# Other SBUF phases for the matmul operands of a feed-forward: slots, weight sums and gated tiles moved by unused columns

## The chip, the cores and the metric

The kernel runs on one core of a Trainium2 chip. The metric is the device time of one execution in microseconds (us). Three runs of the kernel before took 2018.37, 2019.25 and 2019.88 us, so the median is 2019.25 us.

## The reference, cut to what matters

Two layers over 512 tokens of width 1024, in f32. Each layer has a feed-forward, a mixer (a convolution module in layer 0, sparse attention in layer 1), a second feed-forward and a gated embedding; a last norm follows.

```python
def swiglu(x, wg, wu, wd):
    return (jax.nn.silu(x @ wg) * (x @ wu)) @ wd

for i in range(DEPTH):                                   # DEPTH = 2
    x = x + 0.5 * swiglu(rms_norm(x, ffn1_norm[i]), ffn1_w_gate[i], ffn1_w_up[i], ffn1_w_down[i])
    h = rms_norm(x, mix_norm[i])
    x = x + (conformer_conv(h, ...) if i % 2 == 0 else nsa_mixer(h, ...))
    x = x + 0.5 * swiglu(rms_norm(x, ffn2_norm[i]), ffn2_w_gate[i], ffn2_w_up[i], ffn2_w_down[i])
    gate = jax.nn.sigmoid(rms_norm(x, ple_norm[i]) @ ple_w_gate[i])
    x = x + gate * (p[i] @ ple_w_in[i])
return rms_norm(x, final_norm)
```

The gate and up matrices are 1024 x 2816, the down matrix 2816 x 1024; there are four feed-forwards in all.

## The kernel before, in words

**Numbers.** Activations lie transposed: 128 features on the partitions, 512 tokens along the row. An f32 product is made of three matmuls in fp32r: every operand is split into a high part h and a low part l, and `mm3` adds h·h (line L356), h·l (L357) and l·h (L358) in PSUM. In a name like `b<-s,wh` of the profile, `b` is the PSUM bank, the first name after the arrow is the moving operand (the activations, streamed through the array) and the second the stationary one (128x128 weights, loaded into the array ahead of the stream). Weight halves are `wh` and `wl`. A load of weights and a stream of another matmul run at the same time.

**The tiles.**
- `s`: 24 slots of 512 f32 (2048 bytes) in the pool `slots`. They hold the residual stream, and the h and l halves of the normed input of most matrices (`X`).
- `px`: tiles of 1024 f32 in the pool `phase`: in a feed-forward the sums of input quarters (`right_sums`), h in the first half and l in the second; in the gated embedding its normed input.
- `raw`, `rawx`: weights as loaded. `wh`, `wl`: their halves, five buffers of 4096 bytes each, eight 128x128 blocks to a buffer. `s1hl`: h and l of a sum of weights, in one tile. `sq`: other sums of weights.
- `G`: products of gate and up before and after the gate. `hid`: h and l of the gated hidden tiles, the moving operand of the down matrix.

**The feed-forward.** `ffn` works in three parts of 8, 8 and 6 hidden tiles (`PARTS`). The first two hidden tiles of the first part are plain products with 512-wide matmuls (moving `s`). The others go two by two through `pairs`, a Strassen-Winograd scheme with seven products of half size for each of gate and up, all 256 tokens wide. A product is four blocks deep, so 4 x 3 = 12 matmuls; a pair of hidden tiles takes 14 products or 168 matmuls: six products with moving `s` (72 matmuls; products "s" and the first of "d"), six with moving `px` and stationary `wh`/`wl` (72; products "c" and the second of "d"), two with moving `px` and stationary `s1hl` (24; product "e"). The order within a pair is: s, s (both halves), c with T2, e with T1, c with T3, d with B22 (moving `s`), d with T4. There are 3 + 4 + 3 pairs in a feed-forward, 40 in the kernel. After each part the down matrix follows, 512 wide, moving `hid`: 22 x 8 x 3 x 4 = 2112 matmuls.

**Elsewhere** `s` is the moving operand of 512-wide matmuls in the plain products, the convolution's first matrix and the attention's projections, `px` in the gated embedding.

**Order.** A scheduler sets the order of instructions on each engine while the program is built; weights run ahead of the matmuls by five buffers (`HLB`). SBUF addresses come from the pools: each pool lies behind the one opened before it, and within a pool each tag behind the tag first asked for before it. A pool's tile with a new tag therefore moves everything behind it.

Of the kernel before, what the change touches and what calls it, by code (L numbers as in the profile page):

```python
# [11 lines left out]
F32 = mybir.dt.float32  # L12
# [9 lines left out]
TAPS = 31  # L22
X_W1, WARM = 4, 18
OUTS = 2
CONV_FIN = 0
PE_LATE = (3, 4, 5)
FIN_PRI = 100
# [24 lines left out]
G, HPG, HD, KV, QD = 4, 4, 64, 256, 1024  # L52
# [143 lines left out]
class Kern:  # L196
    def __init__(self, ctx, tc, aps):
        self.ctx, self.tc, self.nc = ctx, tc, tc.nc
        self.a = aps
        pool = lambda name, **kw: ctx.enter_context(tc.tile_pool(name=name, **kw))  # L200
        self.cpool = pool("consts", bufs=1)
        self.wpool = pool("weights", bufs=1)
        self.spool = pool("slots", bufs=1)
        self.tiny = pool("tiny", bufs=2)
        self.ppool = pool("ps", bufs=1, space=PSUM)
        self.dpool = pool("dram", bufs=1, space=DRAM)
        self.uid = 0
        self.raw, self.hl, self.sums = {}, {}, {}
        self.unskewed = []
        self.HLB, self.held, self.now = 5, set(), None  # L210
        self.next_raw = self.next_split = 0
# [8 lines left out]
        return self.ptile("t", self.tb, dt=dt)  # L220

    def ptile(self, tag, n, w=512, dt=F32):
        self.uid += 1
        return self.phase.tile([128, w], dt, name=f"{tag}{self.uid}", tag=tag, bufs=n)

# [605 lines left out]
    def conv(self, nxt):  # L831
# [24 lines left out]
        for c in range(KD):  # L856
# [13 lines left out]
            for p, o in ((pa, c), (pg, c + KD)):  # L870
                for k in range(KD):
                    self.mm3(p, self.block(("conv_w_pw1", 0, k, o)), X[k], k == 0, k == KD - 1)
                if c == 1 and p is (pa, pg)[CONV_FIN]:
                    next(fin)
# [501 lines left out]
    def final(self, X, R, Z):  # L1376
# [6 lines left out]
        def norm(hs, squares):  # L1383
# [15 lines left out]
            for m in range(KD):  # L1399
                if m % OUTS == 0:  # L1400
                    pair = self.ptile("hid", HIDS).rearrange("p (m n) -> p m n", n=256)
                x, o = self.xs[m][:, hs], pair[:, m % OUTS]
                if m == OUT_AFTER:
# [3 lines left out]
                with self.tc.issue_after((self.root if m in OUT_POOL else self.vins) if m >= OUT_AFTER else done):  # L1407
                    if m in OUT_POOL:
                        nc.gpsimd.tensor_tensor(o, x, Rf, op=OP.mult)
                    else:  # L1410
                        nc.vector.scalar_tensor_tensor(o, x, self.col("final_norm", m), p, op0=OP.mult, op1=OP.mult)
                if m % OUTS == OUTS - 1:
                    nc.sync.dma_start(out[:, m + 1 - OUTS:m + 1, hs], pair[:, :OUTS])
            yield
# [24 lines left out]

    def run(self):  # L1440
        def phase():
            return self.tc.tile_pool(name="phase", bufs=1, reuse_waits="tile")

        self.zd = [self.dpool.tile([D, S], F32, name=f"z{i}") for i in range(L)]
        self.load_consts()
        for i in range(L):
            self.tb = 4
            with phase() as self.phase:
                if i == 0:
                    self.prep_start("ffn1_norm", 0)  # L1450
                    for k in range(KD):
                        self.parts(k)
                    with self.tc.issue_after(self.parted[0]), self.tc.issue_after(self.parted[1]):
                        for k in range(KD):
                            self.square_sum(k)
                self.ffn(1, i, ("mix_norm", i))
            self.tb = 7 if i == 0 else NTB
            with phase() as self.phase:
                if i == 0:
                    self.conv(("ffn2_norm", i))  # L1460
                    self.bias_tables()
                else:
                    self.nsa(("ffn2_norm", i))
            self.tb = 4
            with phase() as self.phase:
                self.ffn(2, i, ("ple_norm", i))
                self.ple(i, ("ffn1_norm", 1) if i == 0 else ("final_norm", 0))
# [64 lines left out]
```

## Time and profile before

| | |
|---|---|
| time of three runs | 2018.37, 2019.25, 2019.88 us |
| the profiled execution: device time / span | 2018.77 us / 2016.7 us |
| granted TensorE clock, mean | 0.996 |
| TensorE matmul (PE) busy | 1992.7 us, 99% |
| weight load (PEld) busy | 1789.7 us, 89% |
| VectorE (DVE) busy | 1546.0 us, 77% |
| ScalarE (ACT) busy | 1100.5 us, 55% |
| GpSimd (POOL) busy | 330.7 us, 16% |
| DMA | 117 GB/s |

The span is the time from the first to the last instruction of the program; the device time has 2.1 us around it. A matmul's duration in the profile is its modelled way through the array, so that it is longer than its share of the time: successive matmuls overlap. What a matmul costs in a stream is the distance from its start to the next one's start.

### The profile page before, as it was taken

How to read it: one execution, taken by the hardware profiler on the slowest of the kernel's cores; microseconds unless marked ns; L12 is line 12 of the kernel's file. 1: busy time of each engine (PE TensorE's matmuls, PEld its weight loads, DVE VectorE, ACT ScalarE, POOL GpSimd, SP SyncE). 2: the span in 40 equal slices, each digit the busy share in tenths (PEclk: the TensorE clock that was granted, in tenths of full speed). 3: DMA queues.
4: the chain of work that ended last, by engine and by line, in shares of the span. 5: the costliest groups of instructions: out<-in, count | busy, mean ns of one | idle time of the engine just before them, and what ended most of it. 6: DMA issues, size and time to landing. Idle time of an engine off the chain costs nothing.

```text
span 2016.7 us, 32709 instructions
## 1 busy us (share of the span) xinstructions
PE 1992.7 (99%) x12534; PEld 1789.7 (89%) x12534; DVE 1546.0 (77%) x2703; ACT 1100.5 (55%) x1972; POOL 330.7 (16%) x365
## 2 busy tenths in 40 slices
PE   8999999999999999999999999999999999999998
PEld 7989999888789898988999989888888789998987
DVE  8869777795687796777968868646889797786875
ACT  7535445662665363555644535437888665363543
POOL 0000000352300000012000000557666200000022
PEclk9999999999999999999999999999999999999999
DMA  4323323466425244243232322463333023232241
GB/s 170 105 96 104 126 74 105 180 206 202 141 97 166 86 144 136 97 133 118 84 115 95 115 87 90 162 182 116 95 90 104 25 99 120 95 116 94 94 141 59
DMA packets 79483, 235.16 MB, mean 117 GB/s; under 512 B 8848, under 2 KB 16160, under 8 KB 79328
## 3 DMA queue, kind: packets, MB, share of 16 engines
q1 hardware_dynamic: 78368, 230.69, 34.6%
q8 instruction: 98, 1.61, 0.3%
q0 software_dynamic: 816, 2.33, 0.3%
q14 instruction: 57, 0.47, 0.1%
q10 hardware_dynamic: 144, 0.07, 0.0%
HBM read 214.66 MB, written 16.29 MB: 115 GB/s over the span
## 4 chain that ended last, share of the span: by engine, by line
PE 91%; DVE 6%; ACT 2%; issue 1%; DMA 0%; SPq 0%; POOL 0%; DVEq 0%; POOLq 0%; ACTq 0%
PE b L356 28%; PE b L357 27%; PE b L358 27%; PE b L821 2%; PE b L1180 1%; PE b L1244 1%; PE b L1263 1%; PE b L1119 1%; PE b L1264 1%; DVE s L415 1%; DVE t L482 1%; DVE wl L294 1%; DVE px L491 0%; DVE acc L432 0%; DMA raw<-in_w 0%
## 5 line engine op out<-in xcount | busy, mean ns | idle before, releaser
L356 PE MATMUL b<-s,wh 128*128 128x256 f32 (+1 forms) x1408 | 448.8, 320 | 0.6 <-ACT wh L292 0.5
L357 PE MATMUL b<-s,wh 128*128 128x256 f32 (+1 forms) x1408 | 447.5, 318 | 0.9 <-DVE s L415 0.6
L358 PE MATMUL b<-s,wl 128*128 128x256 f32 (+1 forms) x1408 | 446.3, 319 | 0.2 <-DVE wl L294 0.2
L292 ACT ACTIVATE wh<-raw 128x1024 fp32r<-128x1024 f32 (+1 forms) x251 | 263.7, 1054 | 256.5 <-PE b L357 174.1
L357 PE MATMUL b<-px,wh 128*128 128x256 f32 (+1 forms) x1112 | 321.5, 289 | 1.7 <-DVE px L491 1.7
L356 PE MATMUL b<-px,wh 128*128 128x256 f32 (+1 forms) x1112 | 321.4, 290 | 0.7 <-ACT G L503 0.7
L358 PE MATMUL b<-px,wl 128*128 128x256 f32 (+1 forms) x1112 | 321.5, 289 | 0.0
L294 DVE TENSOR_TENSOR wl<-raw,wh 128x1024 fp32r<-128x1024 f32 (+1 forms) x205 | 251.0, 1226 | 68.9 <-ACT wh L292 68.4
L356 PEld LDWEIGHTS b<-s,wh 128*128 128x128 f32 x1408 | 268.3, 191 | 19.2 <-ACT wh L292 1.1
L357 PEld LDWEIGHTS b<-s,wh 128*128 128x128 f32 x1408 | 268.0, 190 | 19.5 <-DVE s L415 1.9
L358 PEld LDWEIGHTS b<-s,wl 128*128 128x128 f32 x1408 | 267.5, 191 | 17.7 <-DVE wl L294 0.5
L358 PE MATMUL b<-hid,wl 128*128 128x512 f32 x704 | 275.3, 393 | 0.0
L357 PE MATMUL b<-hid,wh 128*128 128x512 f32 x704 | 274.5, 391 | 0.0
L356 PE MATMUL b<-hid,wh 128*128 128x512 f32 x704 | 269.7, 390 | 0.0
L294 POOL TENSOR_TENSOR wl<-raw,wh 128x1024 fp32r<-128x1024 f32 (+1 forms) x53 | 128.5, 2431 | 709.8 <-ACT wh L292 709.6
L503 ACT ACTIVATE G<-b 128x256 f32<-128x256 f32 x400 | 145.1, 377 | 141.7 <-PE b L358 122.6
L357 PEld LDWEIGHTS b<-px,wh 128*128 128x128 f32 x1112 | 209.5, 188 | 7.0 <-DVE px L491 2.1
L356 PEld LDWEIGHTS b<-px,wh 128*128 128x128 f32 x1112 | 209.5, 189 | 6.0 <-ACT G L503 1.3
L358 PEld LDWEIGHTS b<-px,wl 128*128 128x128 f32 x1112 | 209.4, 188 | 3.8
L357 PEld LDWEIGHTS b<-hid,wh 128*128 128x128 f32 x704 | 132.2, 188 | 29.4
L356 PEld LDWEIGHTS b<-hid,wh 128*128 128x128 f32 x704 | 132.2, 188 | 28.1
L358 PEld LDWEIGHTS b<-hid,wl 128*128 128x128 f32 x704 | 132.1, 188 | 27.5
(246 smaller groups left out, 3624.4 us busy)
## 6 DMA issues: line engine op xcount, KB each, us to landing
raw<-in_w SPq DMA_DIRECT2D x255, 512.0 KB, 3.3
rawx<-in_w SPq DMA_DIRECT2D x80, 512.0 KB, 3.3
tw<-in_tw SPq DMA_DIRECT2D x20, 576.0 KB, 6.8
skew<-table SPq DMA_DIRECT2D x16, 320.0 KB, 5.8
z<-t SPq DMA_DIRECT2D x16, 256.0 KB, 2.2
hid<-z SPq DMA_DIRECT2D x16, 256.0 KB, 4.1
tt<-skew SPq DMA_DIRECT2D x16, 256.0 KB, 3.0
wr<-in_w SPq DMA_DIRECT2D x8, 512.0 KB, 4.1
```

The lines of the kernel that those rows point to most:

```text
L292: nc.scalar.activation(h[:, c], t[:, c], AF.Copy)
L294: eng.tensor_tensor(l[:, c], t[:, c], h[:, c].bitcast(F32), op=OP.subtract)
L356: mm(out, sh, mh, start=start, stop=False, **how)
L357: mm(out, sh, ml, start=False, stop=False, **how)
L358: self.lastmm = mm(out, sl, mh, start=False, stop=stop, **how).ins
L415: b = nc.vector.scalar_tensor_tensor(view(l), x, g, view(h.bitcast(F32)), op0=OP.mult, op1=OP.subtract)
L482: sub = lambda o, x, y: nc.vector.tensor_tensor(o, x, y, op=OP.subtract)
L503: copy = lambda o, x: nc.scalar.activation(o, x, AF.Copy)
L821: nc.tensor.matmul(p[:, q * SP:q * SP + SP], T[q][:, d * 128:d * 128 + 128], u[:, q, o:o + SP], start=d == 0, stop=d == LAGS - 1)
L1119: nc.tensor.matmul(P[mh][:, :124], w, B[kk // 4][:, kk % 4, :], start=kk == 0, stop=kk == 15)
L1180: nc.tensor.matmul(p[:, :32 - lo + nk], Q, KT[:, i, "sw".index(b), lo:32 + nk], start=i == 0, stop=i == 1)
L1244: nc.tensor.transpose(p[:, a * 128:a * 128 + 128], J[a, b][:, kt * 128:kt * 128 + 128], self.ident)
```

## The change

Unused tiles are allocated in front of four places: 16 columns (64 bytes) ahead of the pool `slots`, 48 columns (192 bytes) ahead of the pools of a phase, and in each phase 16 columns ahead of `s1hl`, 48 ahead of `G` and 48 ahead of `hid`, where these tags occur.

```diff
+PAD_SLOTS, PAD_PHASE = 16, 48
+PADS = {"s1hl": 16, "G": 48, "hid": 48}
...
         self.wpool = pool("weights", bufs=1)
+        pool("gap0", bufs=1).tile([128, PAD_SLOTS], F32, name="gap0")
         self.spool = pool("slots", bufs=1)
         self.tiny = pool("tiny", bufs=2)
+        pool("gap1", bufs=1).tile([128, PAD_PHASE], F32, name="gap1")
...
     def ptile(self, tag, n, w=512, dt=F32):
+        if tag in PADS and tag not in self.padded:
+            self.padded.add(tag)
+            self.phase.tile([128, PADS[tag]], F32, name=f"gap{tag}{self.uid}", tag=f"gap{tag}", bufs=1)
         self.uid += 1
...
         def phase():
+            self.padded = set()
             return self.tc.tile_pool(name="phase", bufs=1, reuse_waits="tile")
```

No instruction is added, removed or moved: the two built programs have the same instructions in the same order with the same waits on all five engines (12,372 on PE's list, 3331 on DVE's, 2425 on ACT's, 977 on SP's, 569 on POOL's). The tiles' start addresses within a partition, modulo 256 bytes, are these (a tile's blocks start at multiples of 512 or 1024 bytes from it, so one number holds for all of them):

| tile | before | after |
|---|---|---|
| `raw`, `wh`, `wl` | 192 | 192 |
| `s` | 192 | 0 |
| `s1hl` | 0 | 64 |
| `hid` | 0 | 192 |
| `px`, `G`, `rawx`, `sq` | 0 | 0 |
| `t` of a feed-forward | 0 | 0 |
| `tw`, `e`, `tt`, `zp`, `q`, `kt` (mixers) | unchanged | unchanged |

Of moving minus stationary address modulo 256, which the prediction calls the distance, this makes:

| matmuls | count | before | after |
|---|---|---|---|
| `s` with `wh`/`wl`, 256 wide | 2880 | 0 | 64 |
| `px` with `wh`/`wl`, 256 wide | 3024 | 64 | 64 |
| `px` with `s1hl`, 256 wide | 960 | 0 | 192 |
| `hid` with `wh`/`wl`, 512 wide | 2112 | 64 | 0 |
| `s` with `wh`/`wl`, 512 wide | 1344 | 0 | 64 |
| `px` with `wh`/`wl`, 512 wide | 312 | 64 | 64 |

## The prediction

> **What bounds the kernel now.** I read the page first: busy times, then the chain that ended last.
>
> ```profile
> PE 1992.7 (99%) x12534; PEld 1789.7 (89%) x12534; DVE 1546.0 (77%) x2703; ACT 1100.5 (55%) x1972; POOL 330.7 (16%) x365
> ...
> PE 91%; DVE 6%; ACT 2%; issue 1%; DMA 0%; SPq 0%; POOL 0%; DVEq 0%; POOLq 0%; ACTq 0%
> ```
>
> TensorE is busy nearly all the time, and 91% of the chain is matmuls. Only what shortens the distance between matmul starts can shorten the kernel by much. Second, one stretch of four pairs in the middle of a feed-forward (columns: stretch and length, then busy us of each engine with its instructions, the clock, DMA share, GB/s).
>
> ```profile
> 144.59:224.23 79.64, 79.64 (x674) 79.63 (x673) 66.70 (x95) 46.51 (x78) 0.00 (x0) 1.00 0.34 113
> ```
>
> PE has no gap in it at full clock; 4 x 168 = 672 matmuls in 79.64 us are 118.5 ns each or 19.9 us per pair. DVE works 66.70 of 79.64 us, 16.7 us per pair, so it would not be the bound before a pair falls under 16.7 us. Third, the groups of matmuls with each shape apart (count, then busy us and mean ns of one).
>
> ```profile
> L356 PE MATMUL b<-px,wh 128*128 128x256 f32 x1008 | 281.0, 280 | 0.7 <-ACT G L503 0.7
> L357 PE MATMUL b<-px,wh 128*128 128x256 f32 x1008 | 280.6, 279 | 1.7 <-DVE px L491 1.7
> L358 PE MATMUL b<-px,wl 128*128 128x256 f32 x1008 | 280.3, 278 | 0.0
> L356 PE MATMUL b<-s,wh 128*128 128x256 f32 x960 | 271.3, 283 | 0.3 <-ACT wh L292 0.3
> L357 PE MATMUL b<-s,wh 128*128 128x256 f32 x960 | 271.1, 283 | 0.0
> L358 PE MATMUL b<-s,wl 128*128 128x256 f32 x960 | 269.9, 283 | 0.0
> L357 PE MATMUL b<-px,s1hl 128*128 128x256 f32 x320 | 90.1, 283 | 0.2 <-DVE px L491 0.2
> L356 PE MATMUL b<-hid,wh 128*128 128x512 f32 x704 | 269.7, 390 | 0.0
> L357 PE MATMUL b<-hid,wh 128*128 128x512 f32 x704 | 274.5, 391 | 0.0
> L358 PE MATMUL b<-hid,wl 128*128 128x512 f32 x704 | 275.3, 393 | 0.0
> L358 PE MATMUL b<-s,wl 128*128 128x512 f32 x448 | 176.4, 394 | 0.2 <-DVE wl L294 0.2
> ```
>
> The same work, 256 columns against 128x128 weights, takes 283 ns at distance 0 (`s` with `wh`, and `px` with `s1hl`) and 279 in the mean at distance 64 (`px` with `wh`). It goes with neither the moving tile nor the weights alone: `px` is at 279 with one and at 283 with the other. The durations hold a constant part, so the price of one is read from the time line instead: starts of the first matmul of runs without a gap, and of the first one behind them (start, duration).
>
> ```profile
> 205.72 0.28 PE L356 MATMUL b<-s,wh 128*128 128x256 f32 x1
> 210.04 0.28 PE L356 MATMUL b<-px,wh 128*128 128x256 f32 x1
> 211.46 0.28 PE L356 MATMUL b<-px,s1hl 128*128 128x256 f32 x1
> 212.77 0.28 PE L356 MATMUL b<-px,wh 128*128 128x256 f32 x1
> 214.13 0.28 PE L358 MATMUL b<-px,s1hl 128*128 128x256 f32 x1
> 215.69 0.28 PE L356 MATMUL b<-px,wh 128*128 128x256 f32 x1
> ```
>
> From 205.72 to 210.04 stand three products of `s`, 36 matmuls: 120.0 ns each. From 210.04 to 211.46 stands one product of T2 (`px`, distance 64), 12 matmuls: 118.3. From 212.77 to 214.13 one product of T3 (`px`, distance 64 too): 113.3. From 214.13 to 215.69 thirteen with `s1hl`: 120.0. So distance 0 has one price, 120.0, and distance 64 has two: a quiet state at 113.3, and a disturbed one at 118.3, taken over behind a run of `s` and lost again behind a run with `s1hl`. The quiet state holds by itself: the last products of the kernel are 256 wide, all `px` at distance 64, and no other distance comes between.
>
> ```profile
> 1986.74 0.28 PE L356 MATMUL b<-px,wh 128*128 128x256 f32 x1
> ...
> 1997.62 0.28 PE L356 MATMUL b<-px,wh 128*128 128x256 f32 x1
> ```
>
> Between these two lie 96 matmuls: 113.3 ns each. And 512 wide, in the down matrix (`hid`, distance 64) and in the convolution's first matrix (`s`, distance 0):
>
> ```profile
> 239.87 0.39 PE L356 MATMUL b<-hid,wh 128*128 128x512 f32 x1
> 249.25 0.39 PE L358 MATMUL b<-hid,wl 128*128 128x512 f32 x1
> 400.00 0.39 PE L356 MATMUL b<-s,wh 128*128 128x512 f32 x1
> 409.98 0.39 PE L358 MATMUL b<-s,wl 128*128 128x512 f32 x1
> ```
>
> 41 steps in 9.38 us are 228.8 ns, 44 steps in 9.98 us are 226.8: here distance 0 is the cheaper one, by 2.0 ns. My reading is that the stream of one matmul and the load of the next one's weights get in each other's way when they start in the same place modulo 256 bytes; with 512 columns the load has time to spare, with 256 it has none.
>
> The Trainium skill speaks against any such effect. "SBUF — State Buffer", section "Who interferes with whom", gives TensorE two independent read ports, one for the moving operand and one for the weight load, and says that "PE and ACT never wait on anyone"; by it the change does nothing and the time stays at 2019. The trace does not agree, with 120.0 against 113.3 ns for the same shape; it is a rival below, with a small chance.
>
> **The change part by part.** Nothing is issued that was not issued before; what changes is the price of matmuls. The profiled execution took 2018.8 us (span 2016.7 and 2.1 around it), 0.5 below the median of the runs shown, and the sum is made against it.
>
> 1. *`s`, 256 wide, 0 to 64* (72 per pair, 2880 in all). Bounds from the rows: 113.3 (quiet) and 118.3 (disturbed), so 6.7 to 1.7 ns less each, 19.3 to 4.9 us in all. The mean row of `px` (279 against 283) lies between, 4 ns less or 116. I take the quiet price for pairs that run without a wait: the state that spoils `px` comes behind runs of `s` at distance 0, and these are gone; all of a pair but "e" is then at one distance, as in the last products.
> 2. *`px` with `wh`, 256 wide, unchanged at 64* (72 per pair). No address changes, but its neighbours do. From its mean of 116 to the quiet 113.3 it gains 2.7 each; if every product falls into the disturbed state it loses 2.3.
> 3. *`px` with `s1hl`, 0 to 192* (24 per pair). No row has a 256-wide stream at 192. Bounds: 113.3 and, at the other end, nothing gained, 120.0; a loss isn't excluded (rival four). I take the middle, 116.5.
> 4. *`hid`, 64 to 0* (2112): 2.0 ns less each, 4.2 us. The bound is nothing gained, as the rows of `s` (394, with waits in them) are no shorter than those of `hid`. *`s` 512 wide, 0 to 64* (1344): 2.0 more each, 2.7 us. Together 1.5 us less.
> 5. *DVE and ACT.* They read and write the moved tiles too, at prices that don't follow the address:
>
> ```profile
> L327 DVE TENSOR_TENSOR sq<-raw,rawx 128x512 f32<-128x512 f32 x80 | 54.7, 684 | 10.8 <-DMA rawx<-in_w 9.6 <-DMA raw<-in_w 1.1
> L331 DVE TENSOR_TENSOR s1hl<-rawx,s1hl 128x512 fp32r<-128x512 f32 x80 | 54.6, 683 | 0.2
> ```
>
> L327 reads at 192 and 0, L331 reads at 0 and 0, and they take the same. I cost this at nothing; the cover is DVE's idle 3.2 us per pair (19.9 less 16.7), which shrinks to about 2.4.
>
> Now by pairs. A pair without waits gains 72 x 6.7 = 0.48 us by `s`, 72 x 2.7 = 0.19 by `px`, 24 x 3.5 = 0.08 with `s1hl`: 0.75 us, and becomes 19.15 us long. That is 28 of the 40 pairs (second and third parts of the four feed-forwards): 21.0 us. The other 12 stand in first parts, where PE waits for the input sums; in the first feed-forward it does so thus (a row of the time line with the idle time and what ended it in brackets, then the window behind it, in which the clock falls to 0.64):
>
> ```profile
> 50.02 0.38 PE L357 MATMUL b<-px,wh 128*128 128x256 f32 x1 [0.83 <-DVE px L491]
> ```
>
> ```profile
> 50.00:54.40 4.40, 4.14 (x20) 3.94 (x21) 4.40 (x8) 1.85 (x5) 0.00 (x0) 0.64 0.00 0
> ```
>
> A wait can throw the stream into either state, so these 12 get the mean price: 72 x 4 ns + 24 x 3.5 ns = 0.37 us each, 4.4 us. Of it 48 x 4 ns in each feed-forward, 0.8 us in all, lie ahead of the first wait for `px` L491 and are eaten by it (DVE is late next, and sets that place as before): 3.6 us remain. Sum: 21.0 + 3.6 + 1.5 = 26.1 us, so 2018.8 - 26.1 = 1992.7, **1993 us**. With the best price everywhere (19.3 + 7.8 by 2880 `px` in the pairs + 6.4 with `s1hl` + 1.5 - 0.8 = 34.2) it is 1984.6.
>
> **The rivals.**
> - *Mean price.* `s` behaves in the mean as `px` does now, the states remain mixed: 2880 x 4 ns + 960 x 3.5 ns + 1.5 - 0.8 = 15.6 us, 2003. For it speaks that T2 and T3 already differ at one distance, so the state depends on what comes before; against it the 96 quiet matmuls.
> - *The disturbed state everywhere.* If `s1hl` at 192 no longer resets the stream, all 5760 run at 118.3: `s` gains 4.9, `px` loses 2880 x 2.3 = 6.6, 1.5 comes from the 512-wide ones: 2019. For it speaks that the only products seen to restore the quiet state are those with `s1hl` at distance 0, which the change removes; against it that a pure run at 64 stays quiet.
> - *No effect of addresses,* that is, the change doesn't do what it is about: prices go with a product's place in the pair, 2019. Against it: `px` at 118.3, 113.3 and 120.0 within 6 us, with only the weights' place and the state of the stream differing.
> - *Slower: cold stretches.* A faster PE overtakes DVE's weight sums in the loops, waits as at 50.02, and the clock drops. That window has 20 matmuls in 4.40 us, where 20 x 118.3 ns are 2.4: 2.0 us an episode. It decides from 13 episodes on (26.1 / 2.0); with 16 of them, in 16 of the 40 pairs, the time is 2025. Against it: DVE needs 16.7 us of a pair of 19.15.
>
> **How the numbers follow.** Chances: quiet 0.50 (own range 1984 to 1999), mean price 0.25 (1999 to 2008), partly disturbed in between 0.04 (2008 to 2015), disturbed everywhere 0.11 (2015 to 2022), no effect 0.05, slower 0.05. The prediction is that of the quiet case. The range 1984 to 2015 holds the first three, 0.79. A measurement of this kernel can tell about 0.2% (4 us) from no change. Faster by more are the first three and a little of the fourth, 0.80; within it most of the fourth and the fifth, 0.15; slower 0.05.
>
> **What would show it.** Right: the four-pair stretch, as long as 79.64 now, takes 76.6 us, PE still full; the row of `s` with `wh` 256 wide falls from 283 to 276-277 and that of `px` with `wh` from 279 towards 276; `hid` falls by 1 to 2 ns and `s` 512 wide rises by as much; `s1hl` falls below 283. Mean price: `s` at 279, `px` still 279, stretch 78.2. Disturbed: `px` rises to 281. Wrong: `s` at 283; more waits of PE for DVE and a mean clock under 0.996; or rows of DVE and ACT that lengthen by tens of ns, which would say that they feel addresses too. I would be most wrong in step 3's hold on steps 1 and 2: a product at 192 that disturbs the stream twice per pair.

## The result, and the profile after

The changed kernel takes 1990.49 us (median of 4 runs, 1990.31 to 1990.73) against 2018.82 for the kernel before (2018.37 to 2019.88): a ratio of 0.9859 [0.9844, 0.9873], 1.4% faster. The prediction was 1993 us, range 1984 to 2015. The profiled execution after took 1990.31 us, so it is 28.5 us shorter than the profiled one before. All times and ratios here are those of executions at full granted clock (0.99 and more); one execution further below, at a mean of 0.653 (2799.81 us), is left out of them.

The page of the kernel after, its head and the shares of the chain that ended last:

```profile
span 1988.2 us, 32709 instructions
...
PE 1961.4 (99%) x12534; PEld 1760.0 (89%) x12534; DVE 1544.6 (78%) x2703; ACT 1099.8 (55%) x1972; POOL 331.0 (17%) x365
...
PE 90%; DVE 6%; ACT 1%; issue 1%; DMA 1%; SPq 0%; POOL 0%; DVEq 0%; ACTq 0%; POOLq 0%
```

The same instructions stand on each engine, DVE and ACT work as long as before, and TensorE is still the bound: PE alone lost 31.3 us. The middle part of the first feed-forward, four pairs again (stretch and length, then busy us of each engine, clock, DMA share, GB/s):

```profile
141.26:217.90 76.64, 76.64 (x674) 76.64 (x673) 66.56 (x95) 46.34 (x78) 0.00 (x0) 1.00 0.35 117
```

PE has no gap in it before or after, and at the same full clock the stretch went from 79.64 to 76.64 us. The groups of matmuls, each shape apart (count, busy us, mean ns of one); `mm3` now has lines L363 to L365:

```profile
L364 PE MATMUL b<-px,wh 128*128 128x256 f32 x1008 | 278.9, 277 | 1.7 <-DVE px L498 1.7
...
L365 PE MATMUL b<-hid,wl 128*128 128x512 f32 x704 | 272.7, 389 | 0.0
...
L363 PE MATMUL b<-s,wh 128*128 128x256 f32 x960 | 265.7, 278 | 1.0 <-ACT wh L299 1.0
...
L365 PE MATMUL b<-s,wl 128*128 128x512 f32 x448 | 176.5, 394 | 0.1
...
L364 PE MATMUL b<-px,s1hl 128*128 128x256 f32 x320 | 88.1, 277 | 0.2 <-DVE px L498 0.2
```

`s` 256 wide fell from 283 to 278 ns, `s1hl` from 283 to 277, `hid` with `wl` from 393 to 389; the row of `s` 512 wide with `wl` stayed at 394, although its matmuls cost 1.5 ns more from start to start; `px` with `wh` fell too, from 279 to 277, though its own address and its weights' address stayed where they were. The wait for `px` is 1.7 us as before.

As in the prediction, a matmul's price is the distance from its start to the next start. Worked out over all matmuls of a kind (steps with a wait left out of the means; "quiet" is the share of steps under 115 ns):

| | before | after | predicted after |
|---|---|---|---|
| `s`, 256 wide | 119.9 ns, distance 0 | 114.7 ns, distance 64, 69% quiet | 113.3 in 28 pairs, 116 in 12 |
| `px` with `wh`/`wl`, 256 wide | 116.1, distance 64, 38% quiet | 114.3, distance 64, 77% quiet | 113.3 in 28 pairs |
| `px` with `s1hl` | 119.7, distance 0 | 113.8, distance 192, 90% quiet | 116.5 |
| `hid`, 512 wide, with `wh` / `wl` | 228.2 / 230.5, distance 64 | 227.0 / 226.8, distance 0 | 2.0 less |
| `s`, 512 wide | 228.0, distance 0 | 229.5, distance 64 | 2.0 more |

### The profile page after: what moved, and what is told of

Its sections match the earlier page's. It is cut to its first block, busy times and chain, and to the rows that moved or that the text cites. A ratio compares the mean times of both kernels' runs of the same rounds, so it can differ in the third digit from the quotient of the medians.

```text
span 1988.2 us, 32709 instructions
## 1 busy us (share of the span) xinstructions
PE 1961.4 (99%) x12534; PEld 1760.0 (89%) x12534; DVE 1544.6 (78%) x2703; ACT 1099.8 (55%) x1972; POOL 331.0 (17%) x365
## 4 chain that ended last, share of the span: by engine, by line
PE 90%; DVE 6%; ACT 1%; issue 1%; DMA 1%; SPq 0%; POOL 0%; DVEq 0%; ACTq 0%; POOLq 0%
PE b L363 27%; PE b L364 27%; PE b L365 27%; PE b L828 2%; PE b L1187 1%; PE b L1251 1%; DMA raw<-in_w 1%; PE b L1270 1%; PE b L1271 1%; PE b L1126 1%; DVE s L422 1%; DVE t L489 1%; DVE wl L301 1%; DVE px L498 0%; DVE acc L439 0%
## 5 line engine op out<-in xcount | busy, mean ns | idle before, releaser
L363 PE MATMUL b<-s,wh 128*128 128x256 f32 (+1 forms) x1408 | 443.8, 316 | 2.2 <-ACT wh L299 1.4
L364 PE MATMUL b<-s,wh 128*128 128x256 f32 (+1 forms) x1408 | 440.9, 314 | 1.4 <-DVE s L422 1.2
L365 PE MATMUL b<-s,wl 128*128 128x256 f32 (+1 forms) x1408 | 440.2, 314 | 0.1
L363 PE MATMUL b<-px,wh 128*128 128x256 f32 (+1 forms) x1112 | 319.4, 288 | 0.7 <-ACT G L510 0.7
L365 PE MATMUL b<-px,wl 128*128 128x256 f32 (+1 forms) x1112 | 319.6, 288 | 0.0
L363 PEld LDWEIGHTS b<-s,wh 128*128 128x128 f32 x1408 | 264.5, 188 | 21.2 <-ACT wh L299 2.2
L364 PEld LDWEIGHTS b<-s,wh 128*128 128x128 f32 x1408 | 264.3, 188 | 20.4 <-DVE s L422 2.3
L365 PEld LDWEIGHTS b<-s,wl 128*128 128x128 f32 x1408 | 263.4, 188 | 18.6 <-DVE wl L301 0.5
L365 PE MATMUL b<-hid,wl 128*128 128x512 f32 x704 | 272.7, 389 | 0.0
L363 PE MATMUL b<-hid,wh 128*128 128x512 f32 x704 | 269.1, 389 | 0.0
L363 PEld LDWEIGHTS b<-px,wh 128*128 128x128 f32 x1112 | 208.4, 188 | 6.1 <-ACT G L510 1.3
L365 PEld LDWEIGHTS b<-px,wl 128*128 128x128 f32 x1112 | 208.8, 188 | 4.0
L365 PEld LDWEIGHTS b<-hid,wl 128*128 128x128 f32 x704 | 132.0, 188 | 27.1
L363 PEld LDWEIGHTS b<-hid,wh 128*128 128x128 f32 x704 | 132.1, 188 | 26.9
```

Source lines behind the costliest of these rows:

```text
L363: mm(out, sh, mh, start=start, stop=False, **how)
L364: mm(out, sh, ml, start=False, stop=False, **how)
L365: self.lastmm = mm(out, sl, mh, start=False, stop=stop, **how).ins
```

## The experiments

**Theory one:** a 256-wide matmul's price goes with its distance (moving minus stationary address modulo 256) and with a state of the stream, quiet or disturbed, which is carried from one matmul to the next. **Rivals:** prices go with the addresses themselves, or with a product's place in the pair; or one of the three moves alone brings everything. All variants of the kernel below have the order of matmuls of the kernel before, and only unused columns differ. An edit is shown against the changed kernel, unless it says otherwise; where both sizes are 0, the tiles `gap0` and `gap1` are left out.

**Each move alone.**

```diff
-PADS = {"s1hl": 16, "G": 48, "hid": 48}
+PADS = {}                                # e_slots: only s moves, to distance 64
```

> Of the change only the slots are moved (s from 192 to 0, so distance 0 to 64); s1hl stays at distance 0 and hid at 64. Theory one (distance with a state): the product with s1hl still takes 120 ns and still leaves the stream quiet, so s falls to about 114.7 and px with wh to about 114.5 as in the changed kernel: 2880 x 5.2 + 2880 x 1.6 less, 1344 x 1.5 more for the 512-wide s, about 2001 us. Rival one (a price per distance and no state): s at px's mean of 116.2, px unchanged, about 2010 us. Rival two (only s1hl at 192 restores the quiet state): s at 118, px up to 118, 2017 to 2020 us.

It took 1995.37 us (1994.52 to 1996.11), ratio 0.9886 [0.9870, 0.9903].

```profile
L363 PE MATMUL b<-s,wh 128*128 128x256 f32 x960 | 265.0, 277 | 0.9 <-ACT wh L299 0.9
...
L364 PE MATMUL b<-px,s1hl 128*128 128x256 f32 x320 | 90.2, 283 | 0.2 <-DVE px L498 0.2
```

`s` fell to 277 and `s1hl` stayed at 283. From start to start, `s` is at 114.0 ns, `px` at 113.9 (86% quiet), `s1hl` at 120.0. That is theory one with more of the quiet state than it counted on: this move alone brings 23.5 us, where 18 were expected.

```diff
-PAD_SLOTS, PAD_PHASE = 16, 48
-PADS = {"s1hl": 16, "G": 48, "hid": 48}
+PAD_SLOTS, PAD_PHASE = 0, 0
+PADS = {"s1hl": 16, "G": 48}             # e_sums: only s1hl moves, to distance 192
+PADS = {"hid": 48}                       # e_hid: only hid moves, to distance 0
```

> Of the change only s1hl is moved (0 to 64, distance of px to it 0 to 192); s stays at distance 0 to its weights and hid at 64. Theory one and a price per distance alike: s1hl 120 to 113.8, 960 x 5.9 = 5.7 us less, 2013 us; with the state taken over from it the px products behind it stay quiet as they are, and those behind s stay at 118. Rival (the address of the moving operand alone counts): px has not moved, 2019 us.

> Of the change only hid is moved (0 to 192, distance 64 to 0). Theory one: the down matrix' 2112 matmuls go from 229.0 to 226.9 ns, 4.4 us less, 2014.4 us; 256-wide products as before (s 119.9, px 116.2). Rival (hid gains nothing by itself, as the duration rows of s 512 wide are no shorter): 2019 us.

`e_sums` took 2013.21 us (2012.34 to 2014.22), ratio 0.9974 [0.9964, 0.9984]; `e_hid` 2014.45 (2013.71 to 2016.48), 0.9980 [0.9970, 0.9989]. Of `e_sums`:

```profile
L361 PE MATMUL b<-s,wh 128*128 128x256 f32 x960 | 271.1, 283 | 0.4 <-ACT wh L297 0.4
...
L362 PE MATMUL b<-px,s1hl 128*128 128x256 f32 x320 | 88.1, 277 | 0.2 <-DVE px L496 0.2
```

Of `e_hid`:

```profile
L363 PE MATMUL b<-hid,wl 128*128 128x512 f32 x704 | 272.7, 389 | 0.0
...
L362 PE MATMUL b<-s,wh 128*128 128x256 f32 x960 | 271.0, 283 | 0.0
```

In each the moved operand alone changed its price, `s1hl` from 119.7 to 113.8 ns and `hid` to 226.9 to 227.0 ns; `s` stayed at 119.9 in both. The three gains, 23.5 + 5.7 + 4.4 = 33.6 us, are more than the 28.3 of all three together: about 5 us are given back when they meet.

**Addresses or distances.** One gap ahead of the weights' pool moves weights and activations alike, so that every address changes by 64 and no distance does (shown against the kernel before).

```diff
+        pool("gap", bufs=1).tile([128, 16], F32, name="gap")
         self.wpool = pool("weights", bufs=1)
```

> The kernel before with everything from the weight buffers on moved by 64 bytes: all addresses differ modulo 256 (wh and wl at 0, s at 0, px, hid and s1hl at 64), all distances are those of before. Theory one (distance): no change, 2019 us, s 256 wide at 120 and px at 116.2. Rival (address alone: moving operands at 0 are cheap and at 192 dear): s is at 0 as in the changed kernel, so 2880 x 5 = 14 us less, 2005 us, and px and hid move away from 0 and may change too.

It took 2019.27 us (2017.96 to 2020.81), ratio 1.0004 [0.9995, 1.0014].

```profile
L363 PE MATMUL b<-px,wh 128*128 128x256 f32 x1008 | 280.1, 278 | 1.6 <-DVE px L497 1.6
...
L362 PE MATMUL b<-s,wh 128*128 128x256 f32 x960 | 271.0, 283 | 0.3 <-ACT wh L298 0.3
```

The rows are those of before. For this shift, it is the distance that counts, not the address.

**Other distances of `s`,** with `s1hl` at 192 and `hid` at 0 as after the change.

```diff
-PAD_SLOTS, PAD_PHASE = 16, 48
+PAD_SLOTS, PAD_PHASE = 48, 16            # e_s192: s at distance 192
+PAD_SLOTS, PAD_PHASE = 32, 32            # e_s128: s at distance 128
```

> The changed kernel with the slots at 128 instead of 0, so s at distance 192 to its weights; everything else as changed. From the run without other engines: 256 wide at 192 is quiet behind 120s and behind s1hl at 192 (113.3), but 117.7 behind the 512-wide run at 0; 512 wide at 192 is 233.4 against 229.5 at 64. Theory one: 1344 x 4 = 5.4 us more by the 512-wide s, 256-wide s and px between quiet everywhere and as now: 1990 to 1997 us. If the change between 192 and 64 within a pair keeps the stream disturbed: up to 2005.

> The changed kernel with the slots at 64 instead of 0, so s at distance 128. From the run without other engines: 118.8 ns at 128, 256 wide, behind any neighbour, and 231.7 to 233.5 ns 512 wide. Theory one: 2880 x 4.1 = 11.8 us more than the changed kernel by s, up to 6 by px that follow s disturbed, 1344 x 3.5 = 4.7 by the 512-wide s: 2007 to 2013 us. Rival (any slot address but 192 will do, since it is enough not to start at the same place): as the changed kernel, 1990.

`e_s192` took 2007.78 us (2007.13 to 2008.49), ratio 0.9950 [0.9935, 0.9965]; `e_s128` 2011.43 (2011.07 to 2013.85), 0.9970 [0.9957, 0.9983]. Of `e_s192`:

```profile
L364 PE MATMUL b<-px,wh 128*128 128x256 f32 x1008 | 280.5, 279 | 1.1 <-DVE px L498 1.1
...
L364 PE MATMUL b<-s,wh 128*128 128x256 f32 x960 | 268.2, 280 | 0.0
...
L365 PE MATMUL b<-s,wl 128*128 128x512 f32 x448 | 178.3, 398 | 0.1
```

Here I missed (1990 to 1997, at most 2005 was expected): a product with `s1hl` at 192 is quiet in the changed kernel, but `s` at 192 is not (117.0 ns, 16 to 19% quiet), and it takes `px` along (116.3). The same product of `s` is quiet or not by what stands around it. At 128, `s` costs 118.7. 512 wide, both cost 232.5 to 233.3 ns, more than the 228.0 at distance 0.

**The kernel without `hid`'s move.**

```diff
-PADS = {"s1hl": 16, "G": 48, "hid": 48}
+PADS = {"s1hl": 16, "G": 48}             # e_nohid
```

> The changed kernel without the move of hid (hid back at 0, distance 64; s at 64 and s1hl at 192 as changed). Theory one: behind hid at distance 0 the run of s begins disturbed (118) in eight of twelve parts until the first product with s1hl, behind hid at 64 it begins quiet; so the down matrix costs 4.4 us more and the 256-wide products some 3 to 6 less: 1989 to 1991.5 us, no slower than the changed kernel at 1990.5. Rival (gains of the three moves add): 4.4 us more, 1995.

It took 1990.12 us (1989.88 to 1991.68), ratio 0.9864 [0.9849, 0.9878]: no slower than with the move. The groups and the middle part of `e_nohid`:

```profile
L365 PE MATMUL b<-hid,wl 128*128 128x512 f32 x704 | 275.9, 394 | 0.0
...
L363 PE MATMUL b<-s,wh 128*128 128x256 f32 x960 | 264.9, 277 | 0.4 <-ACT wh L299 0.4
```

```profile
141.70:218.00 76.30, 76.30 (x674) 76.26 (x674) 66.44 (x95) 46.34 (x78) 0.00 (x0) 1.00 0.36 118
```

`hid` costs 394 ns again, but the four pairs behind it take 76.30 us instead of 76.64. The time lines show where that comes from: starts of the first matmul of the part, of the first with `s1hl` and of the first one behind that. After the change:

```profile
141.26 0.28 PE L363 MATMUL b<-s,wh 128*128 128x256 f32 x1
...
149.74 0.28 PE L363 MATMUL b<-px,s1hl 128*128 128x256 f32 x1
...
152.46 0.28 PE L363 MATMUL b<-px,wh 128*128 128x256 f32 x1
```

In `e_nohid`, the first two of these:

```profile
141.75 0.28 PE L363 MATMUL b<-s,wh 128*128 128x256 f32 x1
...
149.91 0.28 PE L363 MATMUL b<-px,s1hl 128*128 128x256 f32 x1
```

Between the first two starts lie 72 matmuls, all at distance 64. Behind `hid` at 0 they take 8.48 us, 117.8 ns each; behind `hid` at 64 they take 8.16, 113.3 each. The 24 with `s1hl` at 192 that follow take 2.72 us, 113.3 each, and from there on all 576 steps of the part are quiet. All eight second and third parts of the changed kernel go like this: behind `hid` at distance 0 the stream is disturbed, and the first product with `s1hl` heals it. 72 x 4.5 ns are 0.32 us a part, 2.6 us in all eight.

Not every product with `s1hl` at 192 heals, though. In the first part of the fourth feed-forward after the change, the second pair's two begin at the first of these lines and end at the second:

```profile
1642.69 0.28 PE L363 MATMUL b<-px,s1hl 128*128 128x256 f32 x1
...
1645.52 0.28 PE L363 MATMUL b<-px,wh 128*128 128x256 f32 x1
```

These 24 took 117.9 ns each, and the products on both sides of them 117.8; the stream turned quiet only at the third pair's, at 1662.47. What the difference is, the trace doesn't tell. The first parts of `e_nohid` are shorter too, by 1.0 us in the last three feed-forwards. Most of that, 0.8 us, is in the third: behind a wait of 0.24 us for `G` of ACT the stream goes on at 113.3 ns there, and at 117.8 behind the same wait in the changed kernel; why, the traces don't settle.

**All three at distance 64,** the disputed case of the prediction ("a product at 192 that disturbs the stream"), turned round: is it the product at 192 that keeps the stream quiet?

```diff
-PADS = {"s1hl": 16, "G": 48, "hid": 48}
+PADS = {"s1hl": 48, "G": 16}             # e_all64: s, px, s1hl and hid all at 64
```

> s1hl at 192 and hid back at 0: with s at 0 every matmul of the feed-forwards, 256 and 512 wide, stands at distance 64 to its weights, and no product at 192 comes between. Theory one (a state that is taken over, and put right by s1hl at 192): second and third parts as quiet as with hid back alone (76.3 and 57.3 us), but in the first parts a wait of TensorE leaves the stream at 118 and nothing puts it right, so these grow from 63.6 in the mean by up to 72 + 72 + 24 matmuls x 4.5 ns = 0.75 us for each of two to three pairs, 6 to 9 us in all four: 1994 to 1999 us. Rival (one distance everywhere is what keeps it quiet, and the distance of 192 has no part in it): 1989 to 1990.5 us.

It took 2009.46 us (median of six runs, 2003.78 to 2015.52), ratio 0.9956 [0.9942, 0.9971]: the direction of theory one, but a loss of 19 us where it counted on 4 to 9. The six runs spread far wider than the 0.4 us of the changed kernel's four. The same kernel once more, for its profile:

> The kernel with all three right operands 64 from their left ones, once more, for its profile at full clock. By theory one the first product s1hl, now at 64 like its neighbours, no longer brings the stream into the quiet state: s of the later parts and px stay near 116 to 118 ns a step in most products and the time is 2004 to 2015 us. By the rival, that 64 is quiet by itself once s is there, s and px stand at 113.5 to 114.5 ns and the time is 1989 to 1992 us.

One execution, 2017.10 us beside 2017.71 of the kernel before, so still further into the disturbed state than theory one had it (2004 to 2015). Its groups and its middle part:

```profile
L364 PE MATMUL b<-px,wh 128*128 128x256 f32 x1008 | 281.3, 279 | 1.1 <-DVE px L498 1.1
...
L363 PE MATMUL b<-s,wh 128*128 128x256 f32 x960 | 267.5, 279 | 0.4 <-ACT wh L299 0.4
...
L364 PE MATMUL b<-px,s1hl 128*128 128x256 f32 x320 | 88.9, 279 | 0.0
```

```profile
143.70:223.00 79.30, 79.30 (x674) 79.30 (x673) 66.76 (x95) 46.43 (x78) 0.00 (x0) 1.00 0.35 113
```

This is the disturbed state nearly everywhere, which the prediction had as a rival: 672 steps of 117.8 ns in the mean in that part, none under 116. Without the waits `s` won 6.3 us and `px` lost 4.1, the direction of that rival, which had 2019; it measured 2017. Yet the last 96 matmuls of the kernel, also at 64, ran at 113.3 here too. So in this trace a stream at distance 64 stays in the state in which it begins, for hundreds of matmuls, and nothing in it brings the other state back.

It also shows that `hid` at 64 does not make the stream quiet by itself. The part begins, and its first product with `s1hl` follows, at

```profile
143.70 0.28 PE L363 MATMUL b<-s,wh 128*128 128x256 f32 x1
...
152.18 0.28 PE L363 MATMUL b<-px,s1hl 128*128 128x256 f32 x1
```

These 72 matmuls took 117.8 ns each behind `hid` at 64; in `e_nohid`, behind `hid` at 64 too, they took 113.3. Nor need the product that heals be at 192: in the rows that the prediction shows it stood at 0, and in `e_slots`, with `s1hl` at 0 too, `s` and `px` were as quiet as in `e_nohid` (114.0 and 113.9 ns). What these runs show is that with `s1hl` at the same 64 as its neighbours no product with it healed. That the spread of the other runs comes from parts which begin in one state or the other is not shown: they have no trace at full clock.

**No other engine at work.** A kernel of its own runs only matmuls at chosen distances, in runs of 48 or 24, while DVE, ACT and POOL are idle (cut to its loop); it computes none of the reference's work.

```python
def run(n, width, count=RUN):     # M[n]: moving tile n, at its own distance from w; w: eight 128x128 blocks
    for i in range(count):
        nc.tensor.matmul(p[:, :width], w[:, (i % 8) * 128:(i % 8) * 128 + 128], M[n][:, :width], ...)
```

> A kernel of its own, with none of the reference's work: runs of 48 matmuls of fp32r against eight 128x128 weight blocks of one tile, moving operand at 16 distances from the weights (0, 16, ... 240 bytes modulo 256), first 512 columns wide, then 256, while no other engine works; behind them runs of 24 at one distance right behind 24 at another. Theory one (load and stream of TensorE itself collide, by their distance, with a state that is taken over): 256 wide 120 ns from start to start at distance 0, 113.3 at 192, 113.3 or 118 at 64 depending on the run before, 118 behind a run at 0; 512 wide 226.7 at 0, 229 at 64, 233 to 234 at 32 and 160. Rival one (other engines' accesses to SBUF make the difference): all distances alike, 113.3 and 226.7. Rival two (the address of the moving operand alone counts): no theory for the values, but runs behind different neighbours would all have one price per distance.

Its page, a stretch in the middle and five groups (`da` lies at distance 0, `dc` at 64, `df` at 160, `di` at 16):

```profile
PE 405.0 (98%) x2448; PEld 360.2 (87%) x2448; DVE 8.1 (2%) x24; ACT 2.3 (1%) x2; POOL 0.2 (0%) x4
```

```profile
206.00:290.00 84.00, 84.00 (x715) 84.00 (x714) 0.00 (x0) 0.00 (x0) 0.00 (x0) 1.00 0.00 1
```

```profile
L48 PE MATMUL b<-df,w 128*128 128x512 f32 x48 | 11.4, 396 | 0.0
...
L48 PE MATMUL b<-da,w 128*128 128x512 f32 x48 | 11.0, 389 | 0.0
...
L48 PE MATMUL b<-da,w 128*128 128x256 f32 x48 | 5.9, 283 | 0.0
...
L48 PE MATMUL b<-dc,w 128*128 128x256 f32 x48 | 5.8, 279 | 0.0
...
L48 PE MATMUL b<-di,w 128*128 128x256 f32 x48 | 5.6, 276 | 0.0
```

The prices are the large kernel's, with no other engine and no DMA beside them, so contention with DVE, ACT or the weights' transfers isn't their cause. From start to start, in the second half of each run of 48, 256 wide: 120.0 ns at distance 0, 117.7 to 118.7 at 32, 64, 128, 160 and 192, 113.3 at 16 and 112, each behind the run ahead of it; 120.2 at 96 and 119.8 at 80. 512 wide: 226.7 at 0, 228.7 at 64, and 231.0 to 234.8 at the other fourteen multiples of 16. The state is carried here too: distance 192 right behind distance 0 ran at 113.3 after its first few matmuls, behind 160 at 117.8.

## Why the prediction was right

**The effect was the one foretold:** prices go with the distance and with a state carried along. Only matmul distances changed, DVE and ACT were busy as long as before, and the waits hardly grew: nearly the same shares on the chain, TensorE's waits for `wh` of ACT from 0.5 to 1.4 us in all, and the "cold stretches" rival did not occur (clock 0.997). The rival without an effect of addresses fell with `e_micro`, where the same instruction at the same place in its run costs 120.0 or 113.3 ns with nothing changed but the moving tile's address and the run ahead. The four-pair stretch was to take 76.6 us and took 76.64.

**The reading behind it was too simple.** Stream and load were to get in each other's way when they start in the same place modulo 256 bytes. In `e_micro`, 256 wide, distances 96 and 80 are as dear as 0 (120.2 and 119.8 against 120.0 ns), most others lie between, and of the runs of 48 only those at 16 and 112 were quiet; 512 wide, 0 is the cheapest of all. That it is the stream and the load of weights that meet is argued, not shown: no run takes one of them away.

The Trainium skill's rule that stood against it ("SBUF — State Buffer", section "Who interferes with whom": two independent read ports) isn't borne out here. `e_micro` shows the 120.0 against 113.3 ns with nothing but matmuls and their weight loads at work; where on TensorE's way to its operands the price arises, no run tells.

**By its steps** (total us, start to start, waits included; a pair's gain in the prediction was rounded, so the terms add up to 26.4 rather than 26.1):

| step | predicted | measured |
|---|---|---|
| 1, `s` 256 wide | 16.1 less | 346.2 to 331.2: 15.0 less |
| 2, `px` | 5.4 less | 357.4 to 351.2: 6.2 less |
| 3, `s1hl` | 3.4 less | 115.0 to 110.3: 4.7 less |
| 4, `hid` | 4.2 less | 483.7 to 479.3: 4.4 less |
| 4, `s` 512 wide | 2.7 more | 315.1 to 316.2: 1.1 more |

The sum is 29.2 us, against 28.5 by the profiled executions.

- *Steps 1 and 2.* Nearly right, for a reason with a hole in it. The disturbed price, read from 12 starts, was 117.8 and not 118.3. The prediction took the quiet price for all 28 pairs without a wait. In the trace each of the eight second and third parts begins disturbed behind `hid` at 0, 72 matmuls long. By parts: the second ones gained 11.9 us (predicted 16 x 0.75 = 12.0), the third ones 8.4 (12 x 0.75 = 9.0).
- *Step 3* was mis-sized, and it is the step on which the rest hung. I had no row of 192 and took the middle, 116.5; it is 113.8, 5.7 us less without the waits, which makes up for the disturbed starts; that these two misses nearly cancel is luck. More than that, the product with `s1hl` is what heals the stream in the second and third parts, as long as it is not at 64 itself: with it there, 1990 becomes 2004 to 2017. The rival of the disturbed state had that danger right, and gave it to 192; it belongs to 64.
- *Step 4.* `hid` was right on its own and worthless in the sum: its 4.4 us were not costed against what a stream at distance 0 leaves behind, although step 1 had just read that very thing from `s` (118.3 behind a run at distance 0). `e_nohid` gives the same time.
- *The first parts* gained 7.0 us instead of 3.6: the first of them ended at 105.15 before and at 102.18 after, and the other three were 195.66 us long together and are 191.64. One by one they gained 3.0, 2.1, 1.4 and 0.5 us, where 0.9 was counted for each, so the mean price was too careful for three of them and too hopeful for the last. There the stream stayed at 117.8 ns until the third pair's products with `s1hl`, and in the third feed-forward until the second pair's. That their sum beat the forecast owes something to luck.
- *The range* reached to 2015 for the mixed and disturbed cases. Variants fell there: 1995, 2008, 2011 and 2004 to 2017 are what neighbouring distances gave.

No version beat the changed kernel by more than can be measured; `e_nohid` equals it. What `hid` at 0 with a healed start would bring is estimated from the 2.6 us above at 0.13%, and wasn't tried.

## What to carry to other kernels

Where TensorE is full and its matmuls are short (256 columns here), read prices from start to start in runs without a wait, and compare the same shape with different operands: two prices for one shape came from the operands' addresses here, and a few unused columns were worth 1.4%. Test a placement whole, not move by move: prices depended on what ran before, a gain of 4.4 us in one group was given back in the next, and the best distance for 512 columns was nearly the worst for 256. Run a placement several times, too: the changed kernel repeated within 1990.3 to 1990.7 us in four runs, all at distance 64 gave 2004 to 2017 in seven.

## What the runs showed of the hardware that I had not expected

- The preference turns over with the width: distance 0 is the cheapest of sixteen for 512 columns (226.7 ns, others 228.7 to 234.8) and one of the three dearest for 256 (120.0; 96 took 120.2 and 80 119.8).
- At distance 64 both states are stable: 113.3 for 96 matmuls on end, 117.8 for 672 on end, in one execution of `e_all64b`.
- Which state a run takes is not told by its distance alone: 192 was quiet for most of `s1hl` (113.8 in the mean, but 117.9 for 24 on end in one first part), mostly disturbed for `s` (117.0), and 113.3 or 117.8 in `e_micro` by the run ahead. A rule that foretells the state from both was not found, and what makes it stays open.
